# Residual RMSNorm on one core: three 6-row slots in place of two of 8 rows, whole transfers, x queued ahead of the residual

## Chip, cores, metric

The kernel runs on one core of a Trainium2 chip. The metric is device time in microseconds (us), lower is better.

## The reference

Inputs `x` and `residual` are float32 of shape (32, 2048, 2048), `gamma` has 2048 elements.

```python
z = x + residual
rms = np.sqrt(np.mean(z ** 2, axis=-1, keepdims=True) + eps)
return (z / rms * gamma).astype(np.float32)
```

Seen as rows, this is 65,536 rows of 8 KB. Each is read from x, read from residual and written once: 1610.6 MB in all, whatever the kernel does.

## The kernel before

A tile holds 8 rows on each of 128 partitions. x is loaded into one of two slots (64 KB a partition), summed there with the single residual slot, scaled in place and stored from there. All large transfers go through one queue, in order, and an instruction that must wait holds up those behind it. A transfer is issued when the queue hands it to the data engines, and it has landed when its last byte has arrived and its completion is signalled. It is cut into 128 packets, one a partition, 8 for each of the 16 data engines. The queue runs dry when the engines have moved all that was issued.

```python
R = 8; H = R // 2                      # 64 tiles of 128 x 8 rows
# ... cut ...
def load_r(i):
    nc.sync.dma_start(out=r_slot, in_=r_t[i])            # 64 KB a partition

def load_x(i):
    z = z_slots[i % 2]
    for h in range(2):                                   # two halves of 32 KB a partition
        s = slice(h * H, (h + 1) * H)
        nc.sync.dma_start(out=z[:, s, :], in_=x_t[i][:, s, :])
# store(i): whole, except the last tile's, in two halves            ... cut ...

def compute(i):
    for h in range(2):
        nc.vector.tensor_add(...)      # 4 rows: z += residual
        # ScalarE: Square with a row sum, 4 times; then Sqrt of the 4 means
    for h in range(2):
        # VectorE: reciprocal, then 4 times row * rstd * gamma
        ...

load_r(0); load_x(0); load_gamma(); load_x(1); compute(0); load_r(1)
for i in range(1, n_tiles):
    store(i - 1)
    compute(i)
    if i + 1 < n_tiles:
        load_r(i + 1)
        load_x(i + 1)
store(n_tiles - 1)
```

## Time and profile before

| what | value |
|---|---|
| time, median of 3 runs | 3733.61 us (3733.6 to 3735.15) |
| VectorE / ScalarE busy | 62% / 29% |
| moved by the data engines | 1610.63 MB on one queue |
| one 8-row tile in the steady part | 58.06 us for 25.17 MB |

From the page: the busy line of the engines, the two lines on the DMA engines in 40 equal slices of the span (busy tenths, then GB/s), the data queue's line (packets, MB, share of 16 engines' time), and the chain of work that ended last.

```profile
DVE 2298.0 (62%) x772; ACT 1066.4 (29%) x1154; POOL 0.2 (0%) x4
...
DMA  9999999999999999999999999999999999999999
GB/s 425 414 437 430 435 433 431 435 435 432 433 431 435 436 430 437 429 436 433 431 436 430 437 432 431 437 430 439 430 432 434 432 437 431 430 435 436 431 435 389
...
q1 hardware_dynamic: 37008, 1610.63, 99.9%
...
DMA 66%; another core or an unknown queue 16%; DVE 16%; SPq 1%; ACT 0%; issue 0%; DVEq 0%
```

The rate stays near 433 GB/s apart from the first two slices and the last. (Single slices reach 439, because a packet is booked whole in the slice where it starts.) The Trainium skill, "DMA: Bandwidth & Descriptors", section Specifications, gives 435 GB/s as the ceiling of the 16 engines; this trace agrees. So the time of the middle is the bytes divided by the ceiling, and only the ends are left to gain from.

From the costliest groups (busy us and mean ns of one; then the engine's idle time before them): the adds, the squares and the scalings.

```profile
L80 DVE TENSOR_TENSOR z<-z,r_slot 128x8192 f32<-128x8192 f32 x128 | 1112.5, 8692 | 1395.0 <-DMA z<-in_x_dram 1382.5
L83 ACT ACTIVATE sq_junk<-z 128x2048 f32<-128x2048 f32 x512 | 963.5, 1882 | 2635.0 <-DVE z L80 2622.9
L97 DVE SCALAR_TENSOR_TENSOR z<-z,rstd,gamma_tile 128x2048 f32<-128x2048 f32 x512 | 1169.9, 2348 | 4.5
```

The waits of the DMA queue (line and what it waited for: us in total, times, longest). L58 loads the residual, L64 loads x, L69 stores.

```profile
SPq L58 <- DVE rstd L94: 1772.3, 63, 29.3
SPq L58 <- DMA r_slot<-in_residual_dram: 678.5, 62, 12.1
SPq L64 <- DMA out_dram<-z: 625.9, 62, 10.5
SPq L69 <- DVE z L97: 465.1, 63, 18.3
```

These waits sum to 3542 us, and yet the data engines stay busy: a wait of the queue costs time only when everything issued earlier has already been moved. The profile's chain runs through some of these waits (the adds, 16% DVE, and the store that x waits for, most of the 16% "unknown queue"), so a place in the chain alone doesn't show a cost. The timeline of one tile shows that the queue is not dry:

```profile
3575.75 8.69 DVE L80 TENSOR_TENSOR z<-z,r_slot 128x8192 f32<-128x8192 f32 x1 [0.99 <-DMA z<-in_x_dram]
...
3584.47 0.33 SPq L58 DMA_DIRECT2D r_slot<-in_residual_dram  x1
...
3595.08 0.80 SPq L64 DMA_DIRECT2D z<-in_x_dram  x2
```

When the second half of x has landed (3575.75), the previous tile's 8-row store is still queued: 8 packets an engine of 2.418 us, 19.3 us. The residual is issued 8.7 us later, because only the second half's add was left, about 10 us before the queue would have drained.

The windows of the tail (stretch, its length, busy time of each engine, clock, DMA share, GB/s):

```profile
3690.00:3696.00 6.00, 5.01 (x2) 4.07 (x5) 0.00 (x0) 1.00 0.91 393
3696.00:3702.00 6.00, 5.96 (x3) 4.69 (x6) 0.00 (x0) 1.00 1.11 481
3702.00:3708.00 6.00, 6.00 (x3) 5.91 (x7) 0.00 (x0) 1.00 0.23 98
3708.00:3714.00 6.00, 5.96 (x5) 1.96 (x3) 0.00 (x0) 1.00 0.46 197
3714.00:3720.00 6.00, 6.00 (x3) 0.00 (x0) 0.00 (x0) 1.00 1.02 437
```

Most engines are idle from about 3704 to 3711.7, while the last tile is computed. The trace does not name a packet's engine, but each starts where the same engine's last one ended, so the packets can be chained into 16 engines. In that reconstruction most engines wait 6 to 8.5 us here, and the slowest lags the median engine by 7.7 us. As the end comes when the last engine is done, its gap is the one that counts.

### The profile page before, as it was taken

The page shows a single profiled execution, that of the slowest core. Times are in us where ns is not written, and L with a number is a line of the kernel's source. Part 1 is how long each engine was busy: PE and PEld are TensorE (multiplying, and loading weights), DVE is VectorE, ACT ScalarE, POOL GpSimd, SP SyncE. Part 2 cuts the span into 40 slices and gives each one's busy share as a digit, 9 for nine tenths or more (in the row PEclk, how much of TensorE's full clock was granted, in tenths as well). Part 3 has the DMA queues.
Part 4 walks back from the last instruction along what each step waited for, and adds up shares of the span by engine and source line. Part 5 has one row for each costly group of instructions (what it writes and reads, how often), then busy time and mean ns, then how long its engine had stood idle before and what let it go on. Part 6 is the DMA issues. An engine that isn't in the chain of part 4 may idle for free.

```text
span 3732.7 us, 2427 instructions
## 1 busy us (share of the span) xinstructions
DVE 2298.0 (62%) x772; ACT 1066.4 (29%) x1154; POOL 0.2 (0%) x4
## 2 busy tenths in 40 slices
DVE  5665655656557565575655756657566575665756
ACT  2331322313223132231322313323233232331322
POOL 0000000000000000000000000000000000000000
DMA  9999999999999999999999999999999999999999
GB/s 425 414 437 430 435 433 431 435 435 432 433 431 435 436 430 437 429 436 433 431 436 430 437 432 431 437 430 439 430 432 434 432 437 431 430 435 436 431 435 389
DMA packets 37035, 1610.82 MB, mean 432 GB/s; under 512 B 4116, under 2 KB 4116, under 8 KB 4116
## 3 DMA queue, kind: packets, MB, share of 16 engines
q1 hardware_dynamic: 37008, 1610.63, 99.9%
q14 instruction: 19, 0.16, 0.0%
q10 hardware_dynamic: 8, 0.03, 0.0%
HBM read 1073.77 MB, written 536.87 MB: 431 GB/s over the span
## 4 chain that ended last, share of the span: by engine, by line
DMA 66%; another core or an unknown queue 16%; DVE 16%; SPq 1%; ACT 0%; issue 0%; DVEq 0%
DMA z<-in_x_dram 64%; DVE z L80 15%; DMA out_dram<-z 1%; DVE z L97 1%; DMA r_slot<-in_residual_dram 1%; SPq L64 1%; SPq L58 0%; ACT sq_junk L83 0%; DVE rstd L94 0%; DVEq L158 0%; ACT L90 0%; ACT rms L90 0%; DVEq L80 0%
## 5 line engine op out<-in xcount | busy, mean ns | idle before, releaser
L80 DVE TENSOR_TENSOR z<-z,r_slot 128x8192 f32<-128x8192 f32 x128 | 1112.5, 8692 | 1395.0 <-DMA z<-in_x_dram 1382.5
L83 ACT ACTIVATE sq_junk<-z 128x2048 f32<-128x2048 f32 x512 | 963.5, 1882 | 2635.0 <-DVE z L80 2622.9
L97 DVE SCALAR_TENSOR_TENSOR z<-z,rstd,gamma_tile 128x2048 f32<-128x2048 f32 x512 | 1169.9, 2348 | 4.5
L83 ACT ACTIVATION_READ_ACCUMULATOR sq_junk<-z 128x1 f32 x512 | 95.8, 187 | 0.0
L90 ACT ACTIVATE rms<-ssq,eps_tile 128x4 f32<-128x4 f32 x128 | 38.1, 298 | 4.1
L94 DVE RECIPROCAL rstd<-rms 128x4 f32<-128x4 f32 x128 | 21.9, 171 | 0.1
L113 DVE LOAD_MASK_SELECT gamma_tile<-gamma_tile x1 | 0.0, 14 | 21.2 <-DMA gamma_tile<-in_gamma_dram 21.2
L83 ACT ACT_TABLE_LOAD x1 | 1.3, 1283 | 4.4 <-issue 4.4
L113 DVE STREAM_SHUFFLE gamma_tile<-gamma_tile 128x2048 f32<-128x2048 f32 x1 | 2.4, 2419 | 0.0
L108 DVE MEMSET gamma_tile<- 128x2048 f32 x1 | 1.8, 1765 | 0.4 <-issue 0.4
L90 ACT ACT_TABLE_LOAD x1 | 1.3, 1283 | 0.0
L55 DVE MEMSET eps_tile<- 128x1 f32 x1 | 0.1, 59 | 0.8 <-PEq L144 0.8
L144 POOL MEMSET const-bfloat16-1.0<- 128x1 bf16 x1 | 0.1, 103 | 0.0
L144 POOL MEMSET const-uint8-127<- 128x1 uint8 x1 | 0.1, 103 | 0.0
L144 POOL MEMSET const-float32-1.0<- 128x1 f32 x1 | 0.1, 100 | 0.0
L144 POOL MEMSET const-float32-0.0<- 128x1 f32 x1 | 0.1, 99 | 0.2 <-issue 0.2
## 6 DMA issues: line engine op xcount, KB each, us to landing
z<-in_x_dram SPq DMA_DIRECT2D x128, 4096.0 KB, 38.3
out_dram<-z SPq DMA_DIRECT2D x2, 4096.0 KB
r_slot<-in_residual_dram SPq DMA_DIRECT2D x64, 29.9
out_dram<-z SPq DMA_DIRECT2D x63, 50.1
gamma_tile<-in_gamma_dram ACTq DMA_DIRECT2D x4, 8.0 KB
```

The source lines that it names most:

```text
L55: nc.vector.memset(eps_tile, float(eps))
L64: nc.sync.dma_start(out=z[:, s, :], in_=x_t[i][:, s, :])
L80: nc.vector.tensor_add(out=z[:, s, :], in0=z[:, s, :], in1=r_slot[:, s, :])
L83: nc.scalar.activation(out=sq_junk, in_=z[:, h * H + g, :], func=Act.Square, accum_out=ssq[:, g : g + 1],)
L90: nc.scalar.activation(out=rms, in_=ssq, func=Act.Sqrt, bias=eps_tile, scale=inv_d)
L94: nc.vector.reciprocal(out=rstd, in_=rms)
L97: nc.vector.scalar_tensor_tensor(out=row, in0=row, scalar=rstd[:, g : g + 1], in1=gamma_tile, op0=mult, op1=mult,)
L108: nc.vector.memset(gamma_tile, 0.0)
L113: nc.vector.stream_shuffle(gamma_tile, gamma_tile, [0] * 32)
L144: nc = _bacc.Bacc("TRN2", target_bir_lowering=False, num_devices=1)
```

## The change

The intent: a third slot for x, so that its load no longer waits for a store to land; x and residual each in one large transfer; and x ahead of the residual in the queue, since x needs only a free slot. The slots keep the memory that they had, 192 KB a partition: four of 48 KB replace three of 64 KB, so tiles shrink to 6 rows. 85 full tiles and one of 2 rows make up the 512 rows of each partition.

```diff
-    R = 8
-    H = R // 2
+    R = 6
+    NZ = 3
+    n_full = n_rows // (P * R)
+    left = (n_rows - n_full * P * R) // P
+    sizes = [R] * n_full + ([left] if left else [])
 # ... cut ...
-        for h in range(2):
-            s = slice(h * H, (h + 1) * H)
-            nc.sync.dma_start(out=z[:, s, :], in_=x_t[i][:, s, :])
+        nc.sync.dma_start(out=z_slots[i % NZ][:, : sizes[i], :], in_=rows(x_f, i))
 # ... compute: groups of 3 rows in place of 4, otherwise the same ...
-    load_r(0)
+    load_x(0)
-    load_x(0)
+    load_r(0)
 # ...
     for i in range(1, n_tiles):
         store(i - 1)
+        if i + 1 < n_tiles:
+            load_x(i + 1)
         compute(i)
         if i + 1 < n_tiles:
             load_r(i + 1)
-            load_x(i + 1)
```

More of the change, by code (lines that the diff above doesn't have):

```diff
@@ L33, with rows @@
     n_rows, D = x_f.shape
-    R = 8
-    H = R // 2
-    assert n_rows % (P * R) == 0
-    n_tiles = n_rows // (P * R)
-    assert n_tiles >= 3
-    x_t = x_f.rearrange("(n p r) m -> n p r m", p=P, r=R)
-    r_t = r_f.rearrange("(n p r) m -> n p r m", p=P, r=R)
-    o_t = o_f.rearrange("(n p r) m -> n p r m", p=P, r=R)
+    R = 6
+    NZ = 3
+    n_full = n_rows // (P * R)
+    left = (n_rows - n_full * P * R) // P
+    assert n_full * P * R + left * P == n_rows
+    sizes = [R] * n_full + ([left] if left else [])
+    n_tiles = len(sizes)
+    assert n_tiles >= 4
+    def rows(t, i):
+        k = sizes[i]
+        a = i * P * R
+        return t[a : a + P * k, :].rearrange("(p r) m -> p r m", r=k)
     inv_d = 1.0 / float(D)
@@ L48 @@
     psum = ctx.enter_context(tc.tile_pool(name="psum", bufs=1, space=bass.MemoryType.PSUM))
-    z_slots = [slots.tile([P, R, D], fp32, name=f"z{k}") for k in range(2)]
+    z_slots = [slots.tile([P, R, D], fp32, name=f"z{k}") for k in range(NZ)]
     r_slot = slots.tile([P, R, D], fp32, name="r_slot")
@@ L55, with load_x @@
     nc.vector.memset(eps_tile, float(eps))
+    def load_x(i):
+        nc.sync.dma_start(out=z_slots[i % NZ][:, : sizes[i], :], in_=rows(x_f, i))
     def load_r(i):
-        nc.sync.dma_start(out=r_slot, in_=r_t[i])
-    def load_x(i):
-        z = z_slots[i % 2]
-        for h in range(2):
-            s = slice(h * H, (h + 1) * H)
-            nc.sync.dma_start(out=z[:, s, :], in_=x_t[i][:, s, :])
-    def store(i):
-        z = z_slots[i % 2]
-        if i < n_tiles - 1:
-            nc.sync.dma_start(out=o_t[i], in_=z)
-            return
-        for h in range(2):
-            s = slice(h * H, (h + 1) * H)
-            nc.sync.dma_start(out=o_t[i][:, s, :], in_=z[:, s, :])
@@ L75, in compute @@
-    def compute(i):
-        z = z_slots[i % 2]
-        rstds = []
-        for h in range(2):
-            s = slice(h * H, (h + 1) * H)
-            nc.vector.tensor_add(out=z[:, s, :], in0=z[:, s, :], in1=r_slot[:, s, :])
-            ssq = stats.tile([P, H], fp32, name=f"ssq{h}")
-            for g in range(H):
+        nc.sync.dma_start(out=r_slot[:, : sizes[i], :], in_=rows(r_f, i))
+    def store(i):
+        nc.sync.dma_start(out=rows(o_f, i), in_=z_slots[i % NZ][:, : sizes[i], :])
+    def compute(i):
+        z = z_slots[i % NZ]
+        groups = [(a, min(a + 3, sizes[i])) for a in range(0, sizes[i], 3)]
+        rms_of = []
+        for a, b in groups:
+            nc.vector.tensor_add(out=z[:, a:b, :], in0=z[:, a:b, :], in1=r_slot[:, a:b, :])
+            ssq = stats.tile([P, 3], fp32, name=f"ssq{a}")
+            for g in range(a, b):
@@ L83, in compute @@
                 nc.scalar.activation(
                     out=sq_junk,
-                    in_=z[:, h * H + g, :],
+                    in_=z[:, g, :],
                     func=Act.Square,
-                    accum_out=ssq[:, g : g + 1],
+                    accum_out=ssq[:, g - a : g - a + 1],
                 )
-            rms = stats.tile([P, H], fp32, name=f"rms{h}")
-            nc.scalar.activation(out=rms, in_=ssq, func=Act.Sqrt, bias=eps_tile, scale=inv_d)
-            rstds.append((rms, stats.tile([P, H], fp32, name=f"rstd{h}")))
@@ L92, in compute @@
-        for h in range(2):
-            rms, rstd = rstds[h]
-            nc.vector.reciprocal(out=rstd, in_=rms)
-            for g in range(H):
-                row = z[:, h * H + g, :]
+            rms = stats.tile([P, 3], fp32, name=f"rms{a}")
+            nc.scalar.activation(
+                out=rms[:, : b - a],
+                in_=ssq[:, : b - a],
+                func=Act.Sqrt,
+                bias=eps_tile,
+                scale=inv_d,
+            )
+            rms_of.append(rms)
@@ L97, in compute @@
+        for (a, b), rms in zip(groups, rms_of):
+            rstd = stats.tile([P, 3], fp32, name=f"rstd{a}")
+            nc.vector.reciprocal(out=rstd[:, : b - a], in_=rms[:, : b - a])
+            for g in range(a, b):
                 nc.vector.scalar_tensor_tensor(
-                    out=row,
-                    in0=row,
-                    scalar=rstd[:, g : g + 1],
+                    out=z[:, g, :],
+                    in0=z[:, g, :],
+                    scalar=rstd[:, g - a : g - a + 1],
```

## The prediction

> **What bounds it now.** The DMA engines, throughout. The page's slices show DMA at 9 in all 40, mostly 430 to 437 GB/s; the queue part gives 99.9% of 16 engines' span for 1610.63 MB. VectorE is 62% busy, ScalarE 29%. The Trainium skill, "DMA: Bandwidth & Descriptors", section Specifications, puts the ceiling of the 16 engines at 435 GB/s; the trace agrees: one 8-row tile (25.17 MB) takes 58.06 us in the chain of waits near the end, 433.5 GB/s. Sixty-four such tiles are 3716 us of the 3733.
>
> The waits in the DMA queue (29 us for the reciprocal behind the adds, 10 us for a store to land, 7 us for the last scaling) cost nothing: each transfer is still issued 8 to 10 us before the queue drains. The trace's packets show it: between the first 120 us and the last 40 the data engines are idle under 0.15 us per 400 us. Only three places lose time: about 1.7 us at the start, about 1.1 us near 101 us (a residual issued at 100.4, as the queue runs dry), and the tail, where most engines wait 7 to 8.5 us for the last tile's first store. The slowest engine, which lags the others by about 7 us and decides the end, waits only about 1 us there.
>
> **What the change does.** Bytes stay the same. 257 data transfers become 258. Packets per engine: 1040 of 32 KB (median 1.215 us) and 1016 of 64 KB (2.418 us) become 2040 of 48 KB (estimate 1.817 us, halfway) and 24 of 16 KB (0.613 us): 3720.3 us before, 3720.4 after. The rate should hold. DVE and ACT do the same rows: 6-row adds at 6.52 us per 3 rows (three quarters of 8.69), scaling 2.29 us a row.
>
> Steady state after: the period is about 43.5 us a tile (18.87 MB). When a residual lands, a store and an x load (29 us) are queued behind it; the next residual is issued 13.1 us later (two adds) and the store 27 us later. So the queue is 16 us deep instead of 10: slack where nothing was lost.
>
> Start: 12.6 MB precede the first add in both kernels. Residual 1 is issued about when x 1 drains, store 0 about when residual 1 drains: roughly 1.5 us idle, in place of 1.2.
>
> Tail: after the last full residual, 24.3 us of work (store, 2-row x, 2-row residual) is queued, but the store of the last full tile needs two adds and six scalings, 27.1 us, plus about 2.4 us from landing to issue to first byte: about 5 us idle on the slowest engine, in place of 1. The last 2-row tile hides behind that store.
>
> Sum: 3733.6 + 4 + 0.3 = **3738 us**, range 3729 to 3745. Chances: faster by over 2% 0.005, within 2% 0.985, slower by over 2% 0.01.
>
> **What would show it.** Mean GB/s in inner slices unchanged (430 to 437). 48 KB packets at 1.82 us. DVE and ACT busy within 1% of before. The wait of x for a landed store nearly gone. A gap of all engines of about 5 us roughly 25 us before the end, ahead of the last full store. If steady slices rise or fall by 1% or more, the packet estimate is wrong.
>
> **What would make it wrong.** A pitch of 48 KB instead of 64 KB between the partitions' reads in HBM changing the packet time: 1% of it is 37 us. The order of stores and loads changing the lag between engines. The tail being hidden by that lag (then 3733), or the deeper queue removing losses that I counted as lag (then about 3728).

## The result

The kernel after takes 3738.05 us, median of 6 runs (3737.28 to 3738.57), against 3733.80 us for the kernel before over its 6 runs. The ratio is 1.0011, with a 95% interval of 0.9998 to 1.0024: the same within 2%. A second set of 5 runs of the kernel after gave 3737.26 us, beside 3734.33 for before. So two sets put it 3 to 4 us above the kernel before.

From the page of the kernel after, the same lines as before, and the group of the adds:

```profile
DVE 2311.6 (62%) x858; ACT 1078.6 (29%) x1197; POOL 0.2 (0%) x4
...
GB/s 410 429 432 434 433 434 432 435 433 434 433 434 433 433 434 434 433 435 432 434 433 434 434 434 433 434 432 435 432 436 432 435 432 435 433 434 433 435 432 369
...
q1 hardware_dynamic: 37152, 1610.63, 99.7%
...
L76 DVE TENSOR_TENSOR z<-z,r_slot 128x6144 f32<-128x6144 f32 x171 | 1111.7, 6542 | 1385.4 <-DMA r_slot<-in_residual_dram 1385.4
```

The slices say where the 4 us lie. A slice is 93.3 us. The first two sum to 839 GB/s in both kernels, so the start costs nearly the same. The last is 369 in place of 389: 20 GB/s over 93.4 us is 1.87 MB, and at 433 GB/s that is 4.3 us. The inner slices are alike. The bytes of the packets, counted up to a given time, give a finer split for the profiled runs: the kernel after loses 0.6 us more in the first 187 us, gains 2.2 us from there to 3650 us, and loses 5.0 us more in the tail, 3.4 us in all. (In the second set's profile the tail loses 3.4 us and the rest is the same.) Measured from add to add over the inner tiles, a tile took 58.18 us before and 43.61 after, that is 432.6 and 432.8 GB/s.

The waits of the DMA queue, kernel after (L63 loads x, L66 the residual, L69 stores):

```profile
SPq L66 <- DMA r_slot<-in_residual_dram: 1328.1, 85, 31.4
SPq L69 <- DVE z L98: 1183.3, 86, 20.1
SPq L66 <- DVE rstd L96: 1100.7, 83, 13.3
```

The x load does not appear any more: its 625.9 us of waiting for stores are gone, as intended, and nothing came of it. In the kernel before, other transfers were still being moved while x waited.

The windows of the tail, kernel after, and its timeline there:

```profile
3688.00:3694.00 6.00, 6.00 (x2) 0.31 (x1) 0.00 (x0) 1.00 0.99 429
3694.00:3700.00 6.00, 6.00 (x1) 5.90 (x7) 0.00 (x0) 1.00 0.97 418
3700.00:3706.00 6.00, 5.96 (x5) 5.87 (x6) 0.00 (x0) 1.00 0.44 188
3706.00:3712.00 6.00, 5.96 (x5) 0.53 (x3) 0.00 (x0) 1.00 0.10 41
3712.00:3718.00 6.00, 6.00 (x2) 0.00 (x0) 0.00 (x0) 1.00 0.61 262
```

```profile
3687.10 13.03 DVE L76 TENSOR_TENSOR z<-z,r_slot 128x6144 f32<-128x6144 f32 x2 [16.38 <-DMA r_slot<-in_residual_dram]
3693.68 0.33 SPq L66 DMA_DIRECT2D r_slot<-in_residual_dram  x1
...
3714.12 4.41 DVE L76 TENSOR_TENSOR z<-z,r_slot 128x4096 f32<-128x4096 f32 x1
3714.23 13.92 SPq L69 DMA_DIRECT2D out_dram<-z  x2
```

The last full residual has landed at 3687.10. The last full tile is ready for its store at 3714.2, 27.1 us later; the 2-row residual went out at 3693.68. Between about 3702 and 3715 the engines run dry. In the reconstruction by engine, most wait 12 to 14 us there and the slowest 4.2 us (also in the second profile), against none before. That is the size of the whole difference, 3 to 4 us, to within the 1 to 2 us by which start and inner tiles differ.

### The profile page after: what moved, and what is told of

Its sections match the earlier page's. It is cut to its first block, busy times and chain, and to the rows that moved or that the text cites. A ratio compares the mean times of both kernels' runs of the same rounds, so it can differ in the third digit from the quotient of the medians. Undisturbed runs are those within 1.5% of the kernel's fastest.

```text
span 3736.0 us, 2707 instructions
## 1 busy us (share of the span) xinstructions
DVE 2311.6 (62%) x858; ACT 1078.6 (29%) x1197; POOL 0.2 (0%) x4
## 4 chain that ended last, share of the span: by engine, by line
DMA 70%; DVE 30%; issue 0%; ACT 0%; DVEq 0%; SPq 0%
DMA r_slot<-in_residual_dram 70%; DVE z L76 30%; DVE z L98 0%; ACT sq_junk L79 0%; DVE rstd L96 0%; DVEq L160 0%; DVEq L76 0%; SPq L63 0%; ACT rms L86 0%
## 5 line engine op out<-in xcount | busy, mean ns | idle before, releaser
L76 DVE TENSOR_TENSOR z<-z,r_slot 128x6144 f32<-128x6144 f32 x171 | 1111.7, 6542 | 1385.4 <-DMA r_slot<-in_residual_dram 1385.4
L86 ACT ACTIVATE rms<-ssq,eps_tile 128x3 f32<-128x3 f32 x171 | 50.7, 296 | 5.5
L96 DVE RECIPROCAL rstd<-rms 128x3 f32<-128x3 f32 x171 | 29.5, 172 | 5.7 <-ACT rms L86 5.7
```

The costliest lines, as they stand in the source:

```text
L76: nc.vector.tensor_add(out=z[:, a:b, :], in0=z[:, a:b, :], in1=r_slot[:, a:b, :])
L86: nc.scalar.activation(out=rms[:, : b - a], in_=ssq[:, : b - a], func=Act.Sqrt, bias=eps_tile, scale=inv_d,)
L96: nc.vector.reciprocal(out=rstd[:, : b - a], in_=rms[:, : b - a])
```

## The experiments

Ten runs were made, the last of them the kernel after again. All but the first gave correct results. Two numbers are used below for several of them, both worked out from the packets in the trace and averaged over 16 engines: the idle time of an engine between the first and the last data packet of all, and the excess of packets over the median of their size ("slowed packets"). The kernel after has 14.6 us and 7.1 us of these.

### 1. Without arithmetic

```diff
     def compute(i):
-        z = z_slots[i % NZ]
-        # ... adds, squares, scalings ...
+        pass
```

> The kernel after with all arithmetic taken out: the same 258 data transfers in the same order, each store sending out x as it was loaded (a wrong result on purpose). Theory (the data engines are the limit, and compute delays them only in two short places: about 2 us of gaps near the start and about 4 us before the last full store): 3732 us, between 3730 and 3734, so 5 to 7 us under the kernel after. Rival (waits for compute, or engines disturbing the transfers, cost something in every tile): clearly less, 3720 or below.

It took 3725.95 us (ratio to before 0.9978, interval 0.9966 to 0.9991). This missed the expectation by 6 us, in the direction of the rival, though short of its number. The inner slices tell the two apart:

```profile
GB/s 420 433 433 433 432 434 435 432 433 435 432 434 435 432 433 435 432 433 435 432 433 435 432 434 434 432 434 434 432 434 434 432 434 434 432 434 434 432 434 407
```

They are those of the kernel after, so compute costs nothing in the steady part. The difference is at the ends: the first two slices sum to 853 in place of 839, about 3 us where I had counted 2, and the last is 407 in place of 369, about 8 us where I had counted 4. So most of the miss is in the tail. The slowest engine has lost not only its 4.2 us gap there: it ends 4 us after the median engine, where in the kernel after it lagged by 8.7 us before the gap. Why the lag shrinks was not tested. The page of this kernel also counts 2 packets of instruction transfers, where that of after has 20; what they cost was not isolated.

### 2. The small tile first

```diff
-    sizes = [R] * n_full + ([left] if left else [])
+    sizes = ([left] if left else []) + [R] * n_full
-        a = i * P * R
+        a = P * sum(sizes[:i])
```

> The 2-row tile moved from the end to the start, so that a 6-row tile is last. Theory (the tail is the chain of the last full tile against the transfers queued behind its residual): only one 6-row store, 14.5 us, is queued while the chain needs 27.1 us and 2.4 us of latency, so a gap of about 15 us in place of the kernel after's 4; the gaps at the start, about 2 us, go. Sum: 3747 us, between 3744 and 3751. Rival (the 4 us of the kernel after come from the steady part, from 48 KB packets or the queue's order, not from the tail): about 3738.

It took 3742.63 us (ratio to before 1.0024), 4.6 us over the kernel after and below the expected 3744 to 3751.

```profile
GB/s 420 434 432 435 432 434 434 432 436 430 437 430 437 432 434 434 433 434 431 436 431 436 432 434 434 432 435 432 435 431 436 432 434 434 432 434 432 436 431 336
```

In the reconstruction the slowest engine's gap in the tail is 14.0 us, close to the 15 foreseen and 9.8 us more than in the kernel after. As the whole grew by only 4.6 us, about 5 us came back elsewhere, not 2. The start gave about 3.5 of it (first two slices 854 in place of 839): the idle time of the first 120 us falls from 2.0 to 0.4 us, and the slowed packets from 3.6 to 1.6. In the kernel after, the packets of nearly all engines run long by 0.4 to 0.8 us at several moments in and after the gap. So the gap's idle time is not all that goes with it; but slow packets also stand where there is no gap (at 58 us in experiment 1), so it is not shown that the gap causes them. The rest fits a smaller lag: before the tail's gap the slowest engine is 5.9 us behind the median one, 8.7 in the kernel after.

### 3. The small tile first, and the last tile in pieces

```diff
 # besides the edit of experiment 2, for the last tile only:
+        for a in range(0, sizes[i], 2):
+            nc.sync.dma_start(out=r_slot[:, a : a + 2, :], in_=rows(r_f, i)[:, a : a + 2, :])
 # the same for its store, and groups of 2 rows in its compute
```

> The 2-row tile first, and the last 6-row tile's residual, compute and store in three pieces of 2 rows. Theory: the first piece's residual lands 9.7 us before the last one, so its store and the two after it are each issued before the queue drains: no gap in the tail on the slowest engine and none at the start: 3732 us, between 3730 and 3734, as without any compute and 1 to 2 us under the kernel before. Rival (steady part at fault): 3737 or more.

It took 3728.46 us, 5.4 us under the kernel before on the same chip (ratio 0.9986, interval 0.9973 to 0.9998) and 9.6 us under the median of after. The expected 3732 counted 2 us for the start and 4 for the tail. The page's slices:

```profile
GB/s 422 430 436 432 432 436 432 436 433 432 436 433 431 437 432 434 434 432 436 433 432 437 432 432 436 431 435 434 432 436 432 433 436 432 434 434 432 436 432 397
```

The start is up from 839 to 852, about 3 us, and the last slice from 369 to 397, about 6 us. The inner slices are as ever. So with slots, whole transfers and order of the kernel after untouched, a change of the two ends alone brings it from above the kernel before to below. The rival that the steady part is at fault falls. In its tail the slowest engines have no gap, and the last one ends 4 us after the median; what is left over the kernel without arithmetic is 2.5 us. By 0.14% this is the best version found.

### 4. Two slots, program text with x first

```diff
-    NZ = 3
+    NZ = 2
```

> The kernel after with two x/z slots in place of three, order unchanged (x ahead of residual). Theory: the x load at the head of the queue now waits until the store before it has landed, with nothing queued behind that store, so the engines are idle about 2.4 us (landing and issue latency) in each of some 84 tiles: about 3940 us, between 3910 and 3970. Rival (the third slot's worth is small because the engines are saturated anyway): under 3760.

It took 4033.97 us (one run). But it did not test what the text said: the build put the residual ahead of x in the queue, presumably because its x load had to wait for a store (not tested). So x first with two slots stays untested. The traced order was store, residual, x, the same as in experiment 5. The text of a kernel is not the order of its queue; the built program must be looked at.

### 5. Two slots, residual first

```diff
-    NZ = 3
+    NZ = 2
         store(i - 1)
-        if i + 1 < n_tiles:
-            load_x(i + 1)
         compute(i)
         if i + 1 < n_tiles:
             load_r(i + 1)
+            load_x(i + 1)
```

> Two slots of 6 rows, whole transfers, with the residual issued ahead of x, as in the kernel before. Theory: the residual is issued when both adds are done, 13.1 us after x landed plus 2.4 us of latency, while only one 6-row store, 14.5 us, is queued: about 1 us idle in each tile, so about 3820 us, between 3790 and 3850. Rival (the order alone restores the queue's depth): about 3738.

It took 4037.96 us (one run): 300 us over the kernel after, in place of the 80 expected. The direction and the place were right, the size was not. The packets account for the span's increase of 299.8 us: idle time grew by 141.9 us and slowed packets by 157.9 us. Over 84 tiles that is 1.7 us idle, where I had about 1, and another 1.9 us that I had not counted. In every tile the first packet after the dry spell took mostly 2.1 to 2.9 us in place of 1.815, and so did the last load packet before the store, 2.5 to 3.2 us.

### 6. Three slots, residual first

```diff
         store(i - 1)
-        if i + 1 < n_tiles:
-            load_x(i + 1)
         compute(i)
         if i + 1 < n_tiles:
             load_r(i + 1)
+            load_x(i + 1)
```

> The kernel after with its three slots, but the residual issued ahead of x (store, residual, x in the queue, as the built program shows). Theory: the residual waits for both adds at the head of the queue and holds back x behind it, so only one 6-row store lies behind a landed tile and the queue runs dry in every tile, as with two slots: about 4035 us, between 4000 and 4060. Rival (the third slot alone gives the depth, the order is a detail): 3735 to 3745.

It took 4045.36 us (one run), as the theory has it. The third slot alone is worth nothing. Page and timeline of this kernel:

```profile
GB/s 405 403 396 398 394 396 400 398 404 394 399 399 393 399 404 404 397 396 402 393 396 397 403 399 399 401 397 391 401 402 401 398 404 401 393 397 404 398 404 374
...
q1 hardware_dynamic: 37152, 1610.63, 96.1%
```

```profile
2006.47 13.03 DVE L76 TENSOR_TENSOR z<-z,r_slot 128x6144 f32<-128x6144 f32 x2 [19.82 <-DMA z<-in_x_dram]
...
2019.52 0.33 SPq L66 DMA_DIRECT2D r_slot<-in_residual_dram  x1
...
2019.90 0.42 SPq L63 DMA_DIRECT2D z<-in_x_dram  x1
```

x goes out 0.4 us after the residual: its slot had been free, but the residual ahead of it was waiting for both adds, 13.05 us. The Trainium skill, "DMA: Bandwidth & Descriptors", section "Anatomy of one DMA — SWDGE (gpsimd) path", says that a semaphore wait happens on the issuing sequencer before dispatch and not in the DMA engines. The section is about transfers issued from GpSimd; this trace shows the consequence for a queue of SyncE. Here too the growth of the span over after, 307.2 us, is 150.0 us idle and 157.1 us slowed packets.

### 7. Two slots, x in halves

```diff
-    NZ = 3
+    NZ = 2
-        nc.sync.dma_start(out=z_slots[i % NZ][:, : sizes[i], :], in_=rows(x_f, i))
+        for a in range(0, sizes[i], 3):
+            b = min(a + 3, sizes[i])
+            nc.sync.dma_start(out=z_slots[i % NZ][:, a:b, :], in_=rows(x_f, i)[:, a:b, :])
 # and the order of experiment 5
```

> 6-row tiles with two slots, residual ahead of x, and x in two transfers of 3 rows, as the kernel before loads its x. Theory (the halves already give what the third slot gives: the first add is over when the second half lands, so the residual is issued 6.5 us after landing, well inside a 14.5 us store): no dry queue; 680 more packets per engine at 4 to 9 ns each add 3 to 6 us, and the tail's gap goes, since the last full tile's store is ready after about 20 us instead of 27: 3738 us, between 3732 and 3743. Rival (two slots of 6 rows are too few whatever the split): over 3800.

It took 3743.11 us (ratio to before 1.0024), just outside the expected range and 5.9 us over the kernel after in the same rounds. Against experiment 5, only the split of x differs, and it removes 295 us. So the halves of the kernel before already did the work that the third slot does in the kernel after. The extra packets have a median of 0.912 us for 24 KB, so splitting one of 1.815 us adds 9 ns, 6 us over 680; slowed packets add 6 us more (13.5 against 7.3), and the better end takes 5 to 6 back (last slice 399, in place of 374 in experiment 10).

### 8. The kernel before with x whole

```diff
     def load_x(i):
         z = z_slots[i % 2]
+        if 0 < i < n_tiles - 1:
+            nc.sync.dma_start(out=z, in_=x_t[i])
+            return
         for h in range(2):
```

> The kernel before with x loaded in one transfer of 64 KB a partition instead of two of 32 KB, in all tiles but the first and the last. Packets: 520 fewer per engine at about 12 ns of fixed cost each (2 x 1.215 less 2.418 us), which saves about 6 us. But both 8-row adds, 17.4 us, now come after x has landed, and with 2.4 us of latency that is 19.8 us against a store of 19.4 us in the queue: about 0.4 us idle per tile, 25 us in all. Theory: 3752 us, between 3740 and 3770. Rival (fewer and larger transfers are what counts): about 3728.

It took 3987.21 us (ratio 1.0673). The sign was as the theory has it and the rival's 3728 is excluded, but the size was fourteen times mine: 253 us in place of 18. Idle time grew by 142.9 us, 2.3 us for each of the 62 tiles in place of my 0.4, and slowed packets by 115.7 us. A dry queue came with nearly as much again in slow packets as in idle time. I had also left out that the engines are not in step: at 2031 us, when the next residual starts, most engines have waited about 2.6 us, while the slowest is still moving the store. So with two 8-row slots and this order a whole x load is dear; with the third slot it is not, and in 192 KB a partition the third slot needs the smaller tiles.

### 9. The kernel before with everything in halves

```diff
     def load_r(i):
-        nc.sync.dma_start(out=r_slot, in_=r_t[i])
+        for h in range(2):
+            s = slice(h * H, (h + 1) * H)
+            nc.sync.dma_start(out=r_slot[:, s, :], in_=r_t[i][:, s, :])
 # and every store in two halves
```

> The kernel before with residual and stores in halves as well, so that every packet is 32 KB: 3072 of them per engine in place of 1040 of 32 KB and 1016 of 64 KB. Theory (a fixed cost of 12 ns a packet, nothing else): 3746 us, between 3742 and 3750. Rival (size of a packet does not matter between 32 and 64 KB, only the waits do): 3734 or a little less.

It took 3739.10 us (ratio 1.0012), 4.5 us more than the kernel before, where 12 were expected. Packets do have a fixed cost, but it is smaller than I took it to be: the medians here are 1.213 us for 32 KB against 2.418 for 64 KB, 8 ns a packet, and the records of neighbouring packets overlap a little. The start is also better (421 and 432 GB/s in the first slices in place of 425 and 414). The kernel after has 2064 packets an engine and the kernel before 2056, so this cost could not show between them.

### 10. The kernel after again

> The kernel after, unchanged, on the same chip and in the same rounds as the run with two slots and halves, for comparison. Every theory: 3737 to 3739 us.

It took 3737.26 us (3736.65 to 3738.66), ratio to before 1.0008 (0.9996 to 1.0021). This is the companion of experiment 7 and repeats the result.

## Why the prediction was right

- **The engines at their ceiling.** Right. The steady rate is 432.6 GB/s before and 432.8 after.
- **Packets.** Right: 48 KB took 1.815 us (estimated 1.817), 16 KB 0.611 (0.613). Over 2040 packets that is 3 us an engine less than estimated, nearly as much as the whole effect: part of the agreement of 3738 to the microsecond is luck. The change merges two x transfers into one but also shrinks tiles, so 257 large transfers became 258. So "whole transfers" did not bring fewer packets.
- **The third slot.** Right: its slack lies where nothing was lost. Experiments 5, 6 and 7 show that either design keeps the queue filled, x in halves with two slots, or whole x with three slots and x first. Half of either design loses 300 us.
- **The tail, 4 us.** Right in place and size: the slowest engine's gap is 4.2 us where 5 was predicted, and none before, where 1 was. The growth, 4.2, is the 4 of the prediction. Experiments 2 and 3 moved the gap to 14 us and to none. The term that made it 5 is the 2.4 us from landing to first byte. The trace before has 1.0 us from the first issue to the first packet and 1.4 us from the last data packet to the end of the span; here it was 1.3 us (0.5 from the last completion packet to the add, 0.8 from the store's issue to its first packet), and 27.1 + 1.3 - 24.3 is 4.1. One detail differs from the inner tiles, without effect: the 2-row residual was issued 6.6 us after landing, not 13.05, since its rows overlap only the first add.
- **The start, 1.5 us in place of 1.2.** The difference of 0.3 us was nearly right (0.6 by the packets). The size was too small for both, as slowed packets were not counted: in the kernel after, doing away with the gaps brought about 3.5 us. The error cancelled in the prediction, which is luck, and it is a part of the misses of experiments 1, 2 and 3. Slowed packets in every tile, also not counted, are about half of the growth in experiments 5 and 8.
- **What would show it.** VectorE was busy 0.6% more and ScalarE 1.1%, just over the 1% allowed; neither is the limit.
- **The lag of the slowest engine** behind the median one is 7.7 us before and 8.7 after. It was taken as fixed, but it is 5.9 us in experiment 2 and 4 us at the end of experiment 1. That is most of what experiments 1 to 3 gained beyond the expectation. Its cause was not settled.

## What to carry to other kernels

When the DMA engines run at their ceiling, ask of each wait in the queue how much issued work is still ahead of it; if that never runs out, more buffers buy nothing, and only the first and the last tile are left to shape. Order, splitting and number of slots are one design: compare the time from landing to the next issue with the work queued behind the landed transfer, and leave a margin of several us: an expected shortage of about 1 us cost 3.6 us a tile (experiment 5), one of 0.4 us cost 4.1 (experiment 8). At the end, put a small piece where compute is exposed, and enough queued work ahead of it to cover that compute.

## What the Trainium skill lacked or had wrong

- "DMA: Bandwidth & Descriptors" lacks the cost of a queue that runs dry again and again: with 48 KB packets it was 1.7 us of idle time a tile and 1.9 us more in slowed packets, most of them of 2.1 to 3.2 us in place of 1.815. No run here isolates the mechanism.
- The same page, section "Rules for kernel authors", advises coalescing and at least 1 MiB a transfer, and lacks when splitting pays. All transfers of x, residual and output here were 2 MB or more, and between 24 and 64 KB a packet the cost of one more packet was 8 to 9 ns; splitting to keep the queue filled was worth 295 us (experiment 7 against 5).
- "HBM Reference", section "Specifications (TRN2)", gives about 425 GB/s for a core streaming alone; these kernels kept 432.6 to 432.8 GB/s, loads and stores mixed.
- "DMA: Bandwidth & Descriptors", section "Latency and other measured facts", calls engines 7 and 15 usually slower than the others, and puts it down, as a best guess, to transfers issued from GpSimd. No page has such a lag for transfers issued from SP with equal shares: the slowest engine was 7.7 us behind the median before and 8.7 us after, where it decided how much of a gap counted. This trace doesn't name the engine.
